# Sample-group scan step of a hybrid decoder: one decay multiply per half pinned in program order, and wider step spacing

## The chip, the cores and the metric

The kernel runs on one core of a Trainium2 chip. The metric is the device time of one execution in microseconds (us). It is written in a tile language: the program is traced into instructions for five engines, a scheduler then orders each engine's instructions by its own simulation of the time, and each engine works through its queue in that order. TensorE (PE) does matmuls, VectorE (DVE) and ScalarE (ACT) elementwise work, GpSimd (POOL) a little, and SyncE (SP) issues the DMAs.

## The reference

One step of a decoder trunk over 304 tokens: 16 meta tokens and 256 prompt tokens of one sequence, and 8 sample sequences of 4 tokens that carry a state.

```python
h = x + 0.5 * swiglu(rmsnorm(x), w_gu1, w_down1)
u = rmsnorm(h)
a_b, a_c, a_h, z, xbc, dt, g_a, g_b = split(u @ w_in)
y_a = (a_b * causal_conv3(a_c * a_h)) @ w_a_out
xs, bm, cm = split(silu(causal_conv4(xbc) + bias))
# per token t, for each of 32 heads (4 groups share bm, cm):
#   h_t = exp(dt_t * a) * h_{t-1} + dt_t * x_t * bm_t^T ;  y_t = h_t * cm_t
y_b = (rmsnorm_grouped((y + d_skip * xs) * silu(z))) @ w_b_out
h = h + (sigmoid(g_a) * y_a + sigmoid(g_b) * y_b) @ w_o
h = h + 0.5 * swiglu(rmsnorm(h), w_gu2, w_down2)
out = rmsnorm(h)          # and the new convolution and scan states
```

The scan of the 8 sample sequences is where the change lies: old states (8 x 32 heads x 64 x 128 numbers) are read, multiplied by a decay per head and sequence, and an update (an outer product of tokens and `bm`) is added.

## The kernel before, in words

**The weight stream.** All weights are streamed from memory in tiles of 128 x 128, eight tiles to a DMA (`wraw`). Each unit of eight is split into a high part (`whi`, by ACT, L183) and a low part (`wlo`, by DVE, L184), and each tile is used in three matmuls: high by high (L255), high by the low part of the activations (L258), low by high (L259). `PROGRAM`, an order written out by hand, says which tile comes when, and `drive` walks it. The results are named by phase: `ps_g`, `ps_u`, `ps_d` in the two feed-forward parts, and in the token mix `ps_x`, then `ps_ab`, `ps_ac`, `ps_ah`, and `ps_yb` and others later. When a row of `ps_ah` is done DVE multiplies it (`ab`, L530 and L531), convolves it (`cva`, L537, three times) and forms `yat` and `ya` (L544, L545, L548, with ACT between them).

**The scan beside it.** While phases `ab`, `ac`, `ah`, `z` and so on go through PE, two generators trace the scan in small steps: `prompt()` for the prompt's tokens, in eight parts of four heads, and `sample()` for the sample's, in four groups of eight heads, each of two halves (four sequences each). Both stand in a list `side`. After each weight tile `drive` adds `RATE2` = 0.36 to an account and advances one of the generators, in turn, for each whole step in it; a `yield` ends a step. So a `yield` alone issues nothing and only moves what is behind it later in the trace, by about three tiles per turn, twice that with two generators. While `sample()` sets `self.hold`, `prompt()` doesn't advance.

**What `sample()` does.** Per group g: the tokens are turned and scaled (`tokens(g)`: `xst`, `xdts`, `xl`), `diagonal(g)` multiplies a mask by them (L1146, `ms` by `xdts`). Then `cc` and `bm` are copied; eight products of the state tiles `h` with `cc` (both halves; L1183 before, L1185 after); ACT copies the result to `yr`; four transposes of `yr` (`K` by `yr`; L1191, L1194); DVE multiplies by `ec` into `yo` (L1196, L1199). Then for each half q: four decay multiplies `h = h * dec` (128 x 512 each, L1206, L1209), four `up` products into four PSUM tiles (L1220, L1225), four additions `h = up + h` (L1225, L1230), and the new state goes out by DMA (`store`, for the tile of an earlier half) and the one three halves later comes in (`load`). The `up` tiles of j = 1, 2, 3 take three of the four buffers of a PSUM tag "s", which all the scan's products `sps` share; that of j = 0 is in the pool of the weight stream.

**The prompt's products** in the same PSUM buffers: `xr` by `bt` (L1023, L1024), `xl` by `bl` (L1025), transposes of `xs` (L983), `xs` by `h` (L1043), `w` by `xd` (L1049). DVE reads them as `xd` and `xr` (L987), `hf` (L1029, L1031), `t` (L1052) and an update of `xs` (L1058).

**The order of the queues.** The scheduler may move an instruction ahead of others traced before it, but `tc.keep_in_program_order(ins)` holds `ins` behind everything traced ahead of it on its engine. Before the change it is used on PE: for each `up` product and, by `self.pin()`, for the next weight matmul, so that the weight stream can't pass the `up` products.

Of the kernel before, what the change touches and what calls it, by code (L numbers as in the profile page):

```python
# [12 lines left out]
ALU = mybir.AluOpType  # L13
# [695 lines left out]
class Scan:  # L709
# [375 lines left out]
    def sample(self):  # L1085
        nc, K, V, xs = self.nc, self.K, self.V, self.xs
        te, act, dve, pool = nc.tensor, nc.scalar, nc.vector, nc.gpsimd
        ident = K[:, C_ID:C_ID + P]
        NS = NB * NT
        NX = NS + NL  # L1090
        hts = {}

        def load(u):

            if u < 2 * G:
                hts[u] = self.t("h0", [P, 4, 512], bufs=3)
                nc.sync.dma_start(hts[u], self.h0[u // 2, u % 2])

        xst, rep, xt = {}, {}, {}
        yo = self.t("yo", [P, XC, NS])  # L1100
        late = []

        def tokens(g):


            hs = slice(8 * g, 8 * g + 8)

            def turned(src):
                p = self.ps()
                for j in range(4):  # L1110
                    te.transpose(p[:, j * P:(j + 1) * P], src[:, j], ident)
                return p.rearrange("p (h d) -> p h d", h=8)

            def decayed(pv, i, a):
                xr = self.t("xrs", [P, 8, HD], bufs=2, tag="tmp")
                dve.tensor_tensor(out=xr[a], in0=pv[a], op=ALU.mult,
                                  in1=self.dtr[a, i, hs].unsqueeze(2).to_broadcast([a.stop - a.start, 8, HD]))
                return xr.rearrange("p h d -> p (h d)")

            xf = decayed(turned(rep.pop(g)), 3, slice(0, P))  # L1120
            o = xst[g] = self.t("xst", [P, 512], bufs=2, dt=F32R)
            act.activation(o, xf, AF.Copy)
            dve.scalar_tensor_tensor(out=o, in0=xf, scalar=self.kd[:, 0:1], in1=o.bitcast(F32), op0=ALU.mult,
                                     op1=ALU.subtract)
            del xf
            m = self.mixed_rows(self.sp, 4 * g)
            yield
            pv = turned(m)
            del m
            xt[g] = self.t("xdts", [NX, 8, HD])  # L1130
            dve.tensor_tensor(out=xt[g], in0=pv[0:NX], op=ALU.mult,
                              in1=self.dt[0:NX, 2, hs].unsqueeze(2).to_broadcast([NX, 8, HD]))

            while self.xl:
                yield
            xf = decayed(pv, 2, slice(64, P))
            o = self.xl[g] = xlt
            act.activation(o[64:P], xf[64:P], AF.Copy)
            dve.tensor_tensor(out=o[96:P], in0=xf[96:P], in1=o[96:P].bitcast(F32), op=ALU.subtract)
            yield  # L1140

        def diagonal(g):
            pd = self.ps()
            for j in range(8):
                c, k = divmod(j, 2)
                te.matmul(pd[64 * k:64 * k + 64, c * NX:(c + 1) * NX], lhsT=xt[g][:, j],  # L1146
                          rhs=self.ms[:, 8 * g + j], start=True, stop=True)
            yd = self.t("yd", [P, 4, NX], bufs=2)
            act.activation(yd, pd[:, 0:4 * NX].rearrange("p (c t) -> p c t", c=4), AF.Copy)
            self.yd[g] = yd  # L1150

        def store():
            while late:
                u = late.pop()
                nc.sync.dma_start(self.o_hs[u // 2, u % 2], hts.pop(u))
                load(u + 3)

        for u in range(3):
            load(u)

        xlt = self.t("xl", [P, 512], dt=F32R)
        act.activation(xlt[0:64], K[0:64, 0:512], AF.Copy, scale=0.0)
        cc = self.t("cc", [P, 2 * (P + NT)])
        pool.memset(cc, 0.0)
        rep[0] = self.sample_rows(self.sp, 0)
        yield
        yield from tokens(0)
        diagonal(0)
        yield
        for g in range(G):  # L1170
            gs = slice(4 * g, 4 * g + 4)
            act.activation(cc.rearrange("p (q w) -> p q w", q=2)[:, :, 0:P].rearrange("p q (j r) -> p q j r", j=4)
                           [:, :, :, 0:NT],
                           xs[:, XC + G + g, S0:T].rearrange("p (q j t) -> p q j t", q=2, j=4), AF.Copy)
            bm = self.t("bm", [P, 2, P], dt=F32R)
            for q in range(2):
                act.activation(bm[:, q], self.bs[:, g].bitcast(F32), AF.Copy, scale=self.kd[:, 2 + q:3 + q])


            p = self.ps()  # L1180
            for q in range(2):
                for j in range(4):
                    te.matmul(p[32 * j:32 * j + 32], lhsT=cc[:, P * q + 32 * j:P * q + 32 * j + 32],  # L1183
                              rhs=hts[2 * g + q][:, j], start=q == 0, stop=q == 1)
            yr = self.t("yr", [P, 4, P], tag="tmp", bufs=2)  # L1185
            act.activation(yr, p.rearrange("p (c n) -> p c n", c=4), AF.Copy)
            yield
            store()
            p = self.ps()
            for c in range(4):  # L1190
                te.transpose(p[:, c * P:(c + 1) * P], yr[:, c], ident)  # L1191
            del yr
            for q in range(2):
                y, ec = (t[:, gs, 4 * NT * q:4 * NT * (q + 1)].rearrange("p c (b t) -> p c b t", b=4)  # L1194
                         for t in (yo, self.ec))
                dve.tensor_tensor(out=y, in0=p.rearrange("p (c b n) -> p c b n", c=4, b=4)[:, :, :, NT * q:NT * q + NT],  # L1196
                                  in1=ec, op=ALU.mult)
            if g + 1 < G:
                rep[g + 1] = self.sample_rows(self.sp, 4 * g + 4)  # L1199
            yield  # L1200
            for q in range(2):
                ht = hts[2 * g + q]
                for j in range(4):
                    oh = ht[:, j].rearrange("p (h d) -> p h d", h=8)
                    dec = self.dec[:, 8 * g:8 * g + 8, 4 * q + j].unsqueeze(2).to_broadcast([P, 8, HD])
                    dve.tensor_tensor(out=oh, in0=oh, in1=dec, op=ALU.mult)  # L1206
                    if j == 1:
                        yield

                self.hold = True  # L1210
                yield
                store()
                yield

                ps = [(self.pss if j else self.psm).tile([P, 512], F32, name=f"up{g}_{q}_{j}",
                                                        tag="s" if j else "m") for j in range(4)]

                for j in range(3, -1, -1):
                    a = slice(32 * j, 32 * j + 32)
                    ins = te.matmul(ps[j], lhsT=bm[a, q], rhs=xst[g][a], start=True, stop=True)  # L1220
                    self.tc.keep_in_program_order(ins)
                self.pin()
                self.hold = False
                for j in range(3, -1, -1):
                    dve.tensor_tensor(out=ht[:, j], in0=ps[j], in1=ht[:, j], op=ALU.add)  # L1225
                del ps
                yield
                yield
                late.append(2 * g + q)
                if q == 0:  # L1230
                    y = xs[:, gs, S0:T]
                    ds = V[:, V_DS + 4 * g:V_DS + 4 * g + 4].unsqueeze(2).to_broadcast([P, 4, NS])
                    dve.tensor_tensor(out=yo[:, gs], in0=yo[:, gs], in1=self.yd[g][:, :, 0:NS], op=ALU.add)
                    dve.tensor_tensor(out=y, in0=y, in1=ds, op=ALU.mult)
                    dve.tensor_tensor(out=y, in0=y, in1=yo[:, gs], op=ALU.add)
                    self.ready(g)
            if g + 1 < G:
                yield from tokens(g + 1)
                diagonal(g + 1)
                yield  # L1240
        store()
        yield
# [71 lines left out]
```

## Time and profile before

| what | value |
|---|---|
| runs, median of 3 | 886.96 us (886.14 to 887.67) |
| the profiled execution | 886.51 us |
| its span in the profile | 884.7 us |
| mean granted TensorE clock | 0.991 |
| PE busy | 866.3 us (98%) |
| DVE busy | 620.2 us (70%) |
| ACT busy | 491.1 us (56%) |
| POOL busy | 62.3 us (7%) |
| HBM read, written | 145.34 MB, 12.31 MB |

The span is the part of an execution that the profile's instructions cover; the profiled execution's own time is 1.81 us longer than it. PE is counted busy in 98% of the span, so what can be removed without taking matmuls away is in the few places where PE waits, and in stretches where its clock is granted lower than 1. Times within the trace are counted from the start of the span.

### The profile page before, as it was taken

The numbers are of one execution on the slowest core, as the hardware profiler recorded it, in microseconds if no ns is written. First come the engines' busy times: TensorE is split into PE (matmuls) and PEld (weight loads), VectorE is DVE, ScalarE is ACT, GpSimd is POOL, SyncE is SP. The second block draws the span as 40 slices with busy tenths as digits, with TensorE's granted clock in tenths as the row PEclk, the third lists the DMA queues.
The fourth block names the chain that finished last, engine by engine and source line by source line (L and its number), as shares of the span: only waits on it lengthen the run. The fifth ranks groups of instructions, "written<-read, shape, count | busy, mean of one in ns | idle before, by whom it ended". The sixth has DMA issues, their size and how long they took to land.

```text
span 884.7 us, 16212 instructions
## 1 busy us (share of the span) xinstructions
PE 866.3 (98%) x6428; PEld 845.8 (96%) x6428; DVE 620.2 (70%) x1002; ACT 491.1 (56%) x894; POOL 62.3 (7%) x87
## 2 busy tenths in 40 slices
PE   8999999999999999979999999999999999999995
PEld 7999999999999999869898989999999999999995
DVE  6766666554677798789999799796676666665443
ACT  7543434434677877845665676784465444444442
POOL 0000000000012372001000012100000000000000
PEclk9999999999999999989999999999999999999998
DMA  8554545555654655847584846555555555555541
GB/s 297 175 152 157 162 151 165 147 164 157 212 159 143 153 167 173 316 175 267 193 299 144 291 126 241 186 170 187 167 167 154 168 167 169 161 167 164 167 139 54
DMA packets 45851, 158.69 MB, mean 179 GB/s; under 512 B 7168, under 2 KB 9504, under 8 KB 43472
## 3 DMA queue, kind: packets, MB, share of 16 engines
q1 hardware_dynamic: 45344, 157.21, 55.3%
q8 instruction: 50, 0.82, 0.4%
q10 hardware_dynamic: 432, 0.46, 0.2%
q14 instruction: 25, 0.20, 0.1%
HBM read 145.34 MB, written 12.31 MB: 178 GB/s over the span
## 4 chain that ended last, share of the span: by engine, by line
PE 91%; ACT 4%; DVE 3%; issue 1%; DMA 1%; SPq 0%; DVEq 0%; ACTq 0%
PE ps_d L259 5%; PE ps_d L258 5%; PE ps_d L255 5%; PE ps_u L259 5%; PE ps_g L255 5%; PE ps_u L258 5%; PE ps_u L255 5%; PE ps_g L259 5%; PE ps_g L258 5%; PE ps_x L255 3%; PE ps_x L258 3%; PE ps_x L259 3%; PE ps_yb L259 2%; PE ps_yb L255 2%; PE ps_yb L258 2%; PE ps_z L255 2%
## 5 line engine op out<-in xcount | busy, mean ns | idle before, releaser
L184 DVE TENSOR_TENSOR wlo<-wraw,whi 128x1024 fp32r<-128x1024 f32 (+2 forms) x250 | 300.5, 1203 | 190.0 <-ACT whi L183 189.4
L183 ACT ACTIVATE whi<-wraw 128x1024 fp32r<-128x1024 f32 (+2 forms) x250 | 259.6, 1040 | 296.0 <-issue 183.9
L259 PE MATMUL ps_d<-hh,wlo 128*128 128x304 f32 (+1 forms) x352 | 105.6, 300 | 0.0
L255 PE MATMUL ps_d<-hh,whi 128*128 128x304 f32 (+1 forms) x352 | 105.0, 299 | 0.0
L258 PE MATMUL ps_d<-hl,whi 128*128 128x304 f32 (+1 forms) x352 | 104.7, 298 | 0.0
L258 PEld LDWEIGHTS ps_d<-hl,whi 128*128 128x128 f32 x352 | 66.7, 189 | 0.0
L259 PEld LDWEIGHTS ps_d<-hh,wlo 128*128 128x128 f32 x352 | 66.2, 188 | 0.0
L255 PEld LDWEIGHTS ps_d<-hh,whi 128*128 128x128 f32 x352 | 66.1, 188 | 0.0
L255 PE MATMUL ps_x<-unh,whi 128*128 128x304 f32 x192 | 58.9, 309 | 0.5 <-ACT dtraw L739 0.5
L258 PE MATMUL ps_x<-unl,whi 128*128 128x304 f32 x192 | 58.8, 306 | 0.0
L259 PE MATMUL ps_x<-unh,wlo 128*128 128x304 f32 x192 | 58.7, 306 | 0.0
L255 PE MATMUL ps_g<-n1h,whi 128*128 128x304 f32 x176 | 54.0, 307 | 1.4 <-ACT whi L183 1.4
L258 PE MATMUL ps_u<-n1l,whi 128*128 128x304 f32 x176 | 53.6, 304 | 0.0
L255 PE MATMUL ps_u<-n1h,whi 128*128 128x304 f32 x176 | 53.5, 304 | 0.0
L258 PE MATMUL ps_g<-n1l,whi 128*128 128x304 f32 x176 | 53.4, 304 | 0.0
L259 PE MATMUL ps_g<-n1h,wlo 128*128 128x304 f32 x176 | 53.1, 303 | 0.0
L259 PE MATMUL ps_u<-n1h,wlo 128*128 128x304 f32 x176 | 52.9, 302 | 0.0
L259 PE MATMUL ps_g<-n2h,wlo 128*128 128x288 f32 x176 | 52.3, 297 | 0.0
L255 PE MATMUL ps_u<-n2h,whi 128*128 128x288 f32 x176 | 52.2, 297 | 0.0
L259 PE MATMUL ps_u<-n2h,wlo 128*128 128x288 f32 x176 | 52.1, 296 | 0.0
L255 PE MATMUL ps_g<-n2h,whi 128*128 128x288 f32 x176 | 51.9, 295 | 0.0
L258 PE MATMUL ps_u<-n2l,whi 128*128 128x288 f32 x176 | 51.4, 292 | 0.0
(356 smaller groups left out, 2427.1 us busy)
## 6 DMA issues: line engine op xcount, KB each, us to landing
wraw<-wst SPq DMA_DIRECT2D x241, 512.0 KB, 3.6
h<-h SPq DMA_DIRECT2D x8, 1024.0 KB, 7.2
o_hs<-h SPq DMA_DIRECT2D x8, 1024.0 KB, 4.9
acb<-cumd SPq DMA_DIRECT2D x8, 512.0 KB, 5.1
wraw<-wst SPq DMA_DIRECT2D x7, 256.0 KB, 5.6
hd<-h SPq DMA_DIRECT2D x1, 1216.0 KB, 7.2
h<-hd SPq DMA_DIRECT2D x1, 1216.0 KB, 7.5
o_hp<-hf SPq DMA_DIRECT2D x8, 128.0 KB, 3.5
```

The source lines that it names most:

```text
L183: act.activation(hi[:, a:b], r[:, a:b], AF.Copy)
L184: dve.tensor_tensor(out=lo[:, a:b], in0=r[:, a:b], in1=hi[:, a:b].bitcast(F32), op=ALU.subtract)
L255: ins = te.matmul(o, lhsT=wh, rhs=xh, start=first, stop=False)
L258: te.matmul(o, lhsT=wh, rhs=xl, start=False, stop=False)
L259: te.matmul(o, lhsT=wl, rhs=xh, start=False, stop=last)
```

## The change

Two edits in `sample()`. The first decay multiply (j = 0) of each half is pinned on DVE behind everything traced ahead of it, 8 of 32 multiplies in all; the other three of each half are not. And there are more steps: one between `tokens(0)` and `diagonal(0)`, one more behind `diagonal(0)`, and in each of the four groups one between `store()` (behind the copy to `yr`) and the transposes of `yr`.

```diff
         yield from tokens(0)
+        yield
         diagonal(0)
+        yield
         yield
         for g in range(G):
...
             act.activation(yr, p.rearrange("p (c n) -> p c n", c=4), AF.Copy)
             yield
             store()
+            yield
             p = self.ps()
             for c in range(4):
                 te.transpose(p[:, c * P:(c + 1) * P], yr[:, c], ident)
...
                     dec = self.dec[:, 8 * g:8 * g + 8, 4 * q + j].unsqueeze(2).to_broadcast([P, 8, HD])
-                    dve.tensor_tensor(out=oh, in0=oh, in1=dec, op=ALU.mult)
+                    ins = dve.tensor_tensor(out=oh, in0=oh, in1=dec, op=ALU.mult)
+                    if j == 0:
+                        self.tc.keep_in_program_order(ins)
                     if j == 1:
                         yield
```

The number of instructions on each engine stays the same. In the rows below, numbers behind a name count the tiles of that name, `x8` stands for eight instructions in a row, and `up_0_3` is the product of group 0, half 0, j = 3.

PE's queue at group 0 before. These rows stand in one piece between two matmuls of the weight stream:

```order
L1146 MATMUL sps_4180<-ms_3023,xdts_4150 64x48 x8
L1183 MATMUL sps_4227<-h_29_4040,cc_4048 32x512 x4
L1183 MATMUL sps_4227<-h_30_4042,cc_4048 32x512 x4
L1191 MATMUL sps_4271<-K,yr_4236 128x128 x4
L1023 MATMUL sps_4297<-xr_4113,bt_4079 128x256
L1024 MATMUL sps_4297<-xr_4113,bt_4079 128x256
L983 MATMUL sps_4339<-K,xs 128x128 x4
L1220 MATMUL up_0_3_4405<-xst_4097,bm_4224 128x512
L1025 MATMUL sps_4297<-xl_4046,bl_3608 128x256
L1220 MATMUL up_0_2_4404<-xst_4097,bm_4224 128x512
L1220 MATMUL up_0_1_4403<-xst_4097,bm_4224 128x512
L1220 MATMUL up_0_0_4402<-xst_4097,bm_4224 128x512
```

PE's queue after, the first part. It now stands behind 21 matmuls of `ps_ah`, of which the first row shown is the last:

```order
L259 MATMUL ps_ah_4432<-unh,wlo_4310 128x290
L1146 MATMUL sps_4212<-ms_3023,xdts_4150 64x48 x8
L1023 MATMUL sps_4267<-xr_4113,bt_4079 128x256
L1024 MATMUL sps_4267<-xr_4113,bt_4079 128x256
L1185 MATMUL sps_4285<-h_29_4040,cc_4048 32x512 x4
L1185 MATMUL sps_4285<-h_30_4042,cc_4048 32x512 x4
L983 MATMUL sps_4322<-K,xs 128x128 x4
L255 MATMUL ps_ah_4432<-unh,whi_4309 128x290
```

The second part. It follows after 30 more weight matmuls (3 of `ps_ah`, 24 of `ps_ab`, 3 of `ps_ac`), with the product of `xl` by `bl` among them:

```order
L1043 MATMUL sps_4348<-xs,h_53_4265 128x144 x2
L1049 MATMUL sps_4347<-w_4165,xd_4112 64x112 x2
L1049 MATMUL sps_4347<-w_4165,xd_4112 64x144 x2
L1049 MATMUL sps_4347<-w_4165,xd_4112 64x112 x2
L1049 MATMUL sps_4347<-w_4165,xd_4112 64x144 x2
L1194 MATMUL sps_4383<-K,yr_4294 128x128 x4
L1225 MATMUL up_0_3_4521<-xst_4097,bm_4282 128x512
L1225 MATMUL up_0_2_4520<-xst_4097,bm_4282 128x512
L1225 MATMUL up_0_1_4519<-xst_4097,bm_4282 128x512
L1225 MATMUL up_0_0_4518<-xst_4097,bm_4282 128x512
L255 MATMUL ps_ac_4514<-unh,whi_4428 128x290
```

The transposes of `yr` and the `up` products moved 51 weight matmuls later, are still next to each other, and have the products L1043 and L1049 ahead of them, which stood behind them before.

DVE's queue at the same place before:

```order
L1206 TENSOR_TENSOR h_29_4040<-h_29_4040,dec_3029 128x512 x4
L544 TENSOR_TENSOR yat_4366<-ps_ab_4330,cva_4320 128x256
L545 TENSOR_TENSOR yat_4366<-ps_ab_4330,cva_4320 128x32
L1206 TENSOR_TENSOR h_30_4042<-h_30_4042,dec_3029 128x512 x4
L1196 TENSOR_TENSOR yo_4039<-sps_4271,ec_3031 128x4x16 x2
L987 TENSOR_TENSOR xd_4337<-sps_4339,dtt_2896 128x512
L987 TENSOR_TENSOR xr_4338<-sps_4339,dtr_3999 128x512
```

DVE's queue after, from the same `yat`. First the unpinned multiplies and what follows them:

```order
L545 TENSOR_TENSOR yat_4365<-ps_ab_4313,cva_4303 128x32
L548 TENSOR_TENSOR ya<-yat_4365,ya 128x288
L1209 TENSOR_TENSOR h_29_4040<-h_29_4040,dec_3029 128x512 x3
L1209 TENSOR_TENSOR h_30_4042<-h_30_4042,dec_3029 128x512 x3
L987 TENSOR_TENSOR xd_4320<-sps_4322,dtt_2896 128x512
L987 TENSOR_TENSOR xr_4321<-sps_4322,dtr_3999 128x512
L530 TENSOR_TENSOR ab_2513<-ps_ah_4432,act_4424 128x258
L531 TENSOR_TENSOR ab_2513<-ps_ah_4432,act_4424 128x8x4
L184 TENSOR_TENSOR wlo_4475<-wraw_4426,whi_4474 128x1024
L1029 TENSOR_TENSOR hf_4266<-h_53_4265,er_2975 128x256
L184 TENSOR_TENSOR wlo_4511<-wraw_4472,whi_4510 128x1024
L537 SCALAR_TENSOR_TENSOR cva_4468<-ab_2513,V,cva_4468 128x304
```

And directly behind that last row:

```order
L1058 SCALAR_TENSOR_TENSOR xs<-xs,V,sps_4347 128x256 x2
L1031 TENSOR_TENSOR hf_4266<-sps_4267,hf_4266 128x256
L1052 TENSOR_TENSOR t_64_4359<-sps_4348,eb_4232 128x288
L1199 TENSOR_TENSOR yo_4039<-sps_4383,ec_3031 128x4x16 x2
L1209 TENSOR_TENSOR h_29_4040<-h_29_4040,dec_3029 128x512
```

Six of the eight multiplies of group 0 still stand in one run ahead of `xd` and `xr`; the pinned one of the first half stands behind `yo`, and that of the second half 13 rows further on.

## The prediction

> **What bounds the kernel now.** I read the page's busy times and chain of waits first, then PE's waits, then windows around the one long wait, then the rows of PE and DVE in it.
>
> ```profile
> PE 866.3 (98%) x6428; PEld 845.8 (96%) x6428; DVE 620.2 (70%) x1002; ACT 491.1 (56%) x894; POOL 62.3 (7%) x87
> PE 91%; ACT 4%; DVE 3%; issue 1%; DMA 1%; SPq 0%; DVEq 0%; ACTq 0%
> ...
> PE up L1220 <- DVE yo L1196: 4.1, 1, 4.1
> PE ps_g L255 <- ACT whi L183: 1.4, 1, 1.4
> ...
> PE up L1220 <- DVE xr L987: 0.4, 1, 0.4
> ```
>
> PE carries 91% of the chain. Only what lets PE wait less, or run at full clock where it didn't, can bring time. The longest wait of PE is one of 4.1 us: an `up` product of group 0's first half waits for `yo` (its PSUM tile is the one that `yo` reads), and a shorter one waits for `xr`. The 1.4 us belong to the feed-forward part, which the change doesn't touch. So I look at that one place, by windows (PE, PEld, DVE, ACT, POOL busy, granted clock, DMA share, GB/s):
>
> ```profile
> 372.70:385.45 12.75, 6.87 (x51) 3.49 (x50) 12.59 (x24) 5.29 (x14) 1.06 (x1) 0.84 0.41 125
> 378.05:381.46 3.41, 1.43 (x8) 0.74 (x6) 3.38 (x8) 1.75 (x7) 0.00 (x0) 1.00 0.52 181
> 381.46:384.87 3.41, 0.90 (x3) 0.46 (x3) 3.41 (x9) 0.00 (x0) 0.00 (x0) 0.50 0.00 0
> 384.87:388.29 3.42, 3.42 (x14) 2.98 (x15) 3.42 (x9) 0.00 (x0) 0.00 (x0) 0.50 0.11 37
> 283.00:284.00 1.00, 1.00 (x6) 1.00 (x5) 0.00 (x0) 0.99 (x2) 0.00 (x0) 0.50 0.84 344
> 400.00:420.00 20.00, 20.00 (x155) 19.48 (x157) 18.21 (x34) 10.55 (x21) 1.73 (x4) 1.00 0.79 270
> ```
>
> From 372.70 to 385.45 no weight matmul runs, DVE is busy 12.59 of 12.75 us, and from 381.46 to 388.29 the granted clock is 0.50. That is the removable part. The rows of PE that mark it, and prices of the scan's products at full clock from the chain in order of time:
>
> ```profile
> 372.57 0.30 PE L259 MATMUL ps_ac<-unh,wlo 128*128 128x290 f32 x1
> 383.53 0.76 PE L1220 MATMUL up<-xst,bm 32*128 32x512 f32 x1 [4.05 <-DVE yo L1196]
> 384.73 0.79 PE L1220 MATMUL up<-xst,bm 32*128 32x512 f32 x2 [0.44 <-DVE xr L987]
> 385.45 0.61 PE L255 MATMUL ps_ah<-unh,whi 128*128 128x290 f32 x1
> 388.27 0.33 PE L259 MATMUL ps_ah<-unh,wlo 128*128 128x290 f32 x1
> 391.75 0.29 PE L255 MATMUL ps_ab<-unh,whi 128*128 128x288 f32 x1
> 395.34 0.30 PE L255 MATMUL ps_ac<-unh,whi 128*128 128x290 f32 x1
> ...
> 419.87 0.60 PE sps L1146 x16
> 420.83 1.85 PE sps L1183 x16
> 424.05 1.02 PE sps L1049 x16
> 425.67 0.44 PE sps L1191 x4
> 434.74 0.43 PE sps L1023 x2
> 445.61 0.49 PE sps L1043 x4
> ```
>
> In the hole stand diagonal .60, h·cc 1.85, two sets of four transposes .88, xr·bt .86, xl·bl and four `up` products (about .66 by the .44 for four products of that width): 4.85 us of work. So 12.75 − 4.85 = 7.9 us are idle. Behind it, the twelve weight matmuls that start from 385.45 to 388.27 are 2.82 us apart from first to last; 27 matmuls from 391.75 to 395.34 take 3.59, .133 each, so eleven steps would take 1.48: the half clock costs 1.3. Together 9.2 us are the most that this place can give.
>
> **The change, part by part.** DVE's rows at the place, for the walk:
>
> ```profile
> 374.11 1.23 DVE L184 TENSOR_TENSOR wlo<-wraw,whi 128x1024 fp32r<-128x1024 f32 x1
> 375.25 0.53 DVE L537 SCALAR_TENSOR_TENSOR cva<-ab,V,cva 128x304 f32<-128x304 f32 x1
> 375.69 1.22 DVE L184 TENSOR_TENSOR wlo<-wraw,whi 128x1024 fp32r<-128x1024 f32 x1
> 376.94 0.69 DVE L1139 TENSOR_TENSOR xl<-xrs,xl 32x512 fp32r<-32x512 f32 x1
> 377.66 2.50 DVE L1206 TENSOR_TENSOR h<-h,dec 128x512 f32<-128x512 f32 x4
> 380.19 0.42 DVE L544 TENSOR_TENSOR yat<-ps_ab,cva 128x256 f32<-128x256 f32 x1
> 380.75 0.44 ACT L547 ACTIVATE ya<-yat 128x288 fp32r<-128x288 f32 x1 [0.85 <-DVE yat L545]
> 383.04 0.34 DVE L1196 TENSOR_TENSOR yo<-sps,ec 128x64 f32<-128x64 f32 x2
> 383.30 0.68 DVE L987 TENSOR_TENSOR xd<-sps,dtt 128x512 f32<-128x512 f32 x1
> 383.90 0.68 DVE L987 TENSOR_TENSOR xr<-sps,dtr 128x512 f32<-128x512 f32 x1
> 384.50 0.41 DVE L1029 TENSOR_TENSOR hf<-h,er 128x256 f32<-128x256 f32 x1
> 385.43 0.45 DVE L548 TENSOR_TENSOR ya<-yat,ya 128x288 fp32r<-128x288 f32 x1
> 389.93 0.46 DVE L1052 TENSOR_TENSOR t<-sps,eb 128x288 f32<-128x288 f32 x1 [1.52 <-PE sps L1043]
> 391.10 0.87 DVE L1058 SCALAR_TENSOR_TENSOR xs<-xs,V,sps 128x256 f32<-128x256 f32 x2 [0.49 <-PE sps L1049]
> ```
>
> *The pin alone* moves 8 of 32 multiplies. One costs .62 (four in 2.50). In group 0 it takes two of the eight from ahead of `xd` and `xr`: 1.2 us; the other six stay there. The pinned one of half 0 stands behind `yo` and ahead of the first addition, so an addition waits for it, PE doesn't.
>
> *The extra steps* carry most. They let 21 weight matmuls pass ahead of diagonal, and 30 more pass ahead of the transposes of `yr`. PE, walked at .1345 a weight matmul of this stage (between .1325 for `ab` and .137 for the wider ones): 21 from 372.70 to 375.52, diagonal to 376.1, xr·bt to 377.0, h·cc to 378.8, transposes of xs to 379.3, 3 `ah` to 379.7, 24 `ab` and xl·bl to 383.07, 3 `ac` to 383.47, xs·h .49, w·xd 1.02 to 384.98, transposes of `yr` .44 to 385.42 (their PSUM buffer is free when `xr` is done). Then `up` 3 waits for the two updates of `xs` (L1058), `up` 2 for `hf` (L1031), `up` 1 for `t` (L1052), since these three now hold the PSUM buffers; and the pinned weight matmul stands behind them.
>
> When is DVE there? Its rows each overlap the next by some .07 us, so I take distances of starts. The order up to `xl` is the old one: 376.94 to 377.66. `yat` .34 and .10, with its end at 378.18; ACT's half of `ya` .44 and two handovers, to 378.66, for which DVE waits; `ya` .37 to 379.07; six multiplies at .61 to 382.73; `xd` and `xr` 1.2 (383.30 to 384.50) to 383.93; `ab` in two pieces like `yat`, .44, to 384.38; `wlo` 1.14 (374.11 to 375.25) to 385.52; `hf`'s first half .34 to 385.86; a second `wlo` to 387.0; `cva` .45 to 387.45; the two updates of `xs` .87 to 388.32. A wait on DVE costs .15 of handover (`yo` ends at 383.38, `up` starts at 383.53): `up` 3 at 388.47, behind `hf` at 388.8 `up` 2, behind `t` at 389.17 `up` 1, `up` 0 at once. The weight stream resumes at about 389.5.
>
> So the old wait, 7.9 us, is replaced by one of about 3.65: 385.42 to 388.47 in one piece, 3.05, and some .6 between the four `up` products. What is late now is no longer `yo` but the updates of `xs`, behind six multiplies and two `wlo`.
>
> *The sum.* By 389.5 PE has done all that it had done before at 395.34, when the first of the fourth group of three `ac` matmuls started: 5.84 us earlier, with no half clock in the new run. A new half-clock stretch is the one unknown cost. The windows of 3.41 us above show half clock in the window that follows one in which PE was busy 1.43 us, and again behind one with .90. In the same frame the window 384.87 to 388.29 of the new run would have PE busy .55 us, and half clock until 391.70; 2.2 us of weight stream from 389.5 at half clock lose 1.1, the `up` products a little. I take 1.2; its bounds are 0 (the frame lies otherwise, or the wait is too short) and 2.6 (twice the 1.3 seen). Gain 5.84 − 1.2 = 4.6. By sums, (7.9 + 1.3) − (3.65 + 1.2) = 4.35, which agrees.
>
> One rule bears on this: the Trainium skill, "TensorE: Matmul & The Clock Gate", section "HAM oscillation — how this bites in real kernels", wants no idle gap of TensorE above some 3.4 us, after which the clock falls to half. By that rule the new gap of 3.05 us costs no clock, and the gain would be the full 5.8 us.
>
> *Elsewhere* I cost the edits at nothing. In groups 1 to 3 and in the second halves, 38 to 80 rows of PE's queue lie between the transposes of `yr` and `up`, 5 to 10 us at .1325 to .137 each, against some 2.5 us for four multiplies: that cover hides the pinned one, and PE doesn't wait. The next critical `wlo` behind the pinned multiply and the additions is due about 3 us later than DVE reaches it. That cover is not endless: DVE is busy 18.21 of 20 us from 400 to 420. The state's DMAs behind `store()` go out a few tiles later on SP's queue:
>
> ```profile
> h<-h SPq DMA_DIRECT2D x8, 1024.0 KB, 7.2
> ...
> 392.12 0.34 SPq L1097 DMA_DIRECT2D h<-h  x1
> ```
>
> A load lands in 7.2 us; the first one of the scan is issued at 392.12 and read by the eight products of group 1 at 420.83, so some 20 us are to spare, and PE sees none of it.
>
> The profiled execution took 886.51, of which 884.7 is span: 886.51 − 4.6 = 881.9. It lies .45 below the median of 886.96, so the median after is 882.4.
>
> **Rivals.**
>
> *No half clock*: all as above, but the gap of 3.05 us leaves the clock alone: 886.96 − 5.84 = 881.1. For it speaks that the gap is shorter than the one before (4.05 us, and others ahead of it). Against it: at 283 the clock is .50 while PE is busy 1.00 of 1.00 us, so a long gap is not what it takes.
>
> *More gain*: DVE reaches the updates 3 us earlier than I walk, because the matmuls of `xs` by `h` and `w` by `xd` or the `wlo` come in another rhythm. Idle 1 us: 886.96 − 8.2 = 878.7. Against it: every price in DVE's walk has a row, and DVE has next to no idle time there.
>
> *Nothing comes of it*: what the change takes from DVE's queue is small, two multiplies, and the wait only moves from `yo` to the updates of `xs`. If DVE is 3 to 5 us later than walked (another `wlo` waits for its `whi`, or ACT's `ya` is late, with all six multiplies behind it), `up` starts at 392 to 393 and the gain is within 1.8 us of nothing: 885.2 to 888.7.
>
> *Slower*: the later groups have the same new order, and each stalls as group 0 does in its new place: 3.65 idle and 1.2 of clock, 4.85 each. With one, 886.96 − 4.6 + 4.85 = 887.2, the same as before; from the second on it is slower, 892.1. It decides where DVE falls behind by more than the 2 to 4 us that I count as cover at each such place. For it: 18.21 of 20 us busy. Against it: there, 38 to 80 rows of PE lie between, none in group 0.
>
> **The numbers.** The forecast, gain by a new, shorter wait with some half clock (881.7 to 884.2), has .55; without half clock .17; more gain .04; nothing or one later stall .14; two or more .10. A change of this kernel under 0.2% (1.8 us) can hardly be told from none, so faster means below 885.2 and slower above 888.7: .76, .14, .10. The range is 880.2 to 886.0: it leaves out the larger gain, most of the cases without gain and the slower ones, and takes in both bounds of the clock, 881.1 and 883.7, with about 2 us for DVE's walk on the side where it may be late and 1 us on the other.
>
> **What would show it.** Right: PE's waits list an `up` of about 3 us for the update of `xs`, L1058 (or `hf`, `t`), in place of 4.1 for `yo`; the stream of weights runs from 372.7 with no hole to about 385; `up` 0 is done at about 389.5; the granted clock is .50 for one window near 388 to 392; groups 1 to 3 have no new waits of PE above .5 us. Wrong: `up` later than 391 (DVE's walk failed), no half clock (the clock term), or PE waits for `wlo` or `up` behind 400 (the cover failed).

## The result, and the profile after

| kernel | median | runs | mean granted clock of the runs |
|---|---|---|---|
| before (with the change's own runs) | 886.71 us | 10 (885.23 to 887.67) | .991 over 43 runs of all comparisons |
| after | 881.65 us | 10 (879.43 to 884.48) | .995 (.991 to .998) |

The ratio is 0.9947, 95% interval 0.9933 to 0.9962: a gain of 0.4 to 0.7%, or 5.1 us by the medians. The forecast was 882.4 within 880.2 to 886.0. Measured once more beside other kernels (below), the changed kernel took 882.19 us against 885.84, a ratio of 0.9965 (0.9951 to 0.9980), and the forecast, a ratio of 0.9949, lies between these two; in us it is a little above both medians after. The profiled execution took 880.99 us, 5.52 less than the profiled one of before.

The page's busy times and the engines' shares of the chain after; then the waits of PE:

```profile
PE 863.8 (98%) x6428; PEld 843.6 (96%) x6428; DVE 619.8 (70%) x1002; ACT 491.7 (56%) x894; POOL 63.8 (7%) x87
...
PE 94%; DVE 2%; ACT 2%; issue 1%; DMA 1%; SPq 0%; POOLq 0%; POOL 0%; DVEq 0%; ACTq 0%
```

```profile
PE up L1225 <- DVE xs L1058: 2.4, 1, 2.4
...
PE sps L1043 <- ACT h L1028: 1.2, 1, 1.2
PE ps_g L255 <- ACT whi L183: 1.2, 1, 1.2
```

The span fell from 884.7 to 879.2. PE's time outside its busy rows fell by 3.0 us (18.4 to 15.4), its busy time by 2.5, in part because matmuls at half clock count as busy for longer. The wait for `yo` is gone, and in its place stands one of 2.4 us for the update of `xs`. A wait of 1.2 us is new; it lies at the end of the scan. The same windows as before, cut at the new hole (PE, PEld, DVE, ACT, POOL busy, granted clock, DMA share, GB/s):

```profile
372.70:385.45 12.75, 12.75 (x114) 10.17 (x112) 12.12 (x22) 6.62 (x13) 2.58 (x2) 1.00 0.42 125
385.45:388.89 3.44, 1.09 (x6) 0.55 (x5) 3.44 (x9) 3.43 (x10) 1.08 (x1) 1.00 0.71 189
388.89:396.00 7.11, 7.11 (x54) 7.00 (x52) 7.11 (x16) 3.72 (x11) 0.20 (x1) 1.00 0.65 251
400.00:420.00 20.00, 20.00 (x171) 17.46 (x170) 19.30 (x36) 14.75 (x35) 0.94 (x4) 1.00 0.84 301
```

Where PE had been busy 6.87 of 12.75 us, it is busy throughout; the hole is at 385.45, and in this execution the clock is 1.00 in it and behind it. PE's and DVE's rows at the place:

```profile
384.84 0.66 PE L1194 MATMUL sps<-K,yr 128*128 128x128 f32 x4
387.85 1.11 PE L1225 MATMUL up<-xst,bm 32*128 32x512 f32 x4 [2.35 <-DVE xs L1058]
388.89 0.40 PE L255 MATMUL ps_ac<-unh,whi 128*128 128x290 f32 x1
...
559.75 0.76 PE L1043 MATMUL sps<-xs,h 128*128 128x144 f32 x4 [1.20 <-ACT h L1028]
```

```profile
376.41 0.69 DVE L1139 TENSOR_TENSOR xl<-xrs,xl 32x512 fp32r<-32x512 f32 x1
378.54 3.70 DVE L1209 TENSOR_TENSOR h<-h,dec 128x512 f32<-128x512 f32 x6
382.15 0.69 DVE L987 TENSOR_TENSOR xd<-sps,dtt 128x512 f32<-128x512 f32 x1
...
386.38 0.54 DVE L537 SCALAR_TENSOR_TENSOR cva<-ab,V,cva 128x304 f32<-128x304 f32 x1
386.82 0.88 DVE L1058 SCALAR_TENSOR_TENSOR xs<-xs,V,sps 128x256 f32<-128x256 f32 x2
```

Against the walk: transposes of `yr` at 384.84 (walk 384.98), `up` 3 at 387.85 (388.47), the stream again at 388.89 (389.5). DVE was .5 ahead of the walk from `xl` on (376.41, walk 376.94), and stayed so. That lead is not of the change: the first of the transposes that read `mrows` (L1111), which stand ahead of the place in both orders, starts at 370.26 in this trace and at 370.78 in that of before. In a second profile of the changed kernel (below) it starts at 370.76, and there the transposes of `yr` come at 385.35, `up` 3 at 388.37 and the stream at 389.41. So DVE's part was walked right to .1 us, and PE came to the wait some .4 us later than walked, which makes the wait shorter.

### The profile page after: what moved, and what is told of

It reads as the page before. It is cut to its first block, busy times and chain, and to the rows that moved or that the text cites. A ratio compares the mean times of both kernels' runs of the same rounds, so it can differ in the third digit from the quotient of the medians.

```text
span 879.2 us, 16209 instructions
## 1 busy us (share of the span) xinstructions
PE 863.8 (98%) x6428; PEld 843.6 (96%) x6428; DVE 619.8 (70%) x1002; ACT 491.7 (56%) x894; POOL 63.8 (7%) x87
## 4 chain that ended last, share of the span: by engine, by line
PE 94%; DVE 2%; ACT 2%; issue 1%; DMA 1%; SPq 0%; POOLq 0%; POOL 0%; DVEq 0%; ACTq 0%
PE ps_d L259 6%; PE ps_d L258 5%; PE ps_d L255 5%; PE ps_u L259 5%; PE ps_g L255 5%; PE ps_u L258 5%; PE ps_u L255 5%; PE ps_g L259 5%; PE ps_g L258 5%; PE ps_x L255 3%; PE ps_x L258 3%; PE ps_x L259 3%; PE ps_yb L259 2%; PE ps_yb L255 2%; PE ps_yb L258 2%; PE ps_z L255 2%
```

## The experiments

Theory: the extra steps carry the gain, by letting weight matmuls pass ahead of products that wait for DVE; DVE's chain up to the update of `xs` sets what is left; the half clock behind a hole is a cost of its own. Rivals: the pin carries it; the half clock comes by itself; what is won is given back later. Each kernel was timed beside the kernel before on the same chip. The last column of the table below is 230 us less PE's busy time in the one window that holds the whole scan, from the profile of each kernel. The rows of that window, of before, where they give 6.3 us, and then of the full change, 3.6:

```profile
370.00:600.00 230.00, 223.73 (x1745) 207.58 (x1744) 205.44 (x366) 147.36 (x298) 19.87 (x24) 0.99 0.62 209
```

```profile
370.00:600.00 230.00, 226.37 (x1781) 211.08 (x1780) 208.06 (x372) 150.22 (x301) 22.72 (x23) 1.00 0.63 212
```

(A matmul that runs at half clock or waits for its operand within its row counts as busy, so this is less than the waits worked out by the prices of the products: 7.9 us in the one hole of before.)

The column "place" is the time from the first transpose of `mrows` to the start of the last matmul of `ps_yb`, behind the scan, in the same profile. By the traces every kernel has the same 2030 or 2031 matmuls there (18 more in the filled one), so it leaves out what differs elsewhere; before it is 267.8 us, with the full change 262.9. What lies ahead of it is the same program in all kernels, yet the profiles come to its start between 367.9 and 371.1 us. The medians hold such differences too, and one profile of a kernel doesn't tell whether they come by chance.

| kernel | median us | before, us | ratio (95% interval) | place, us | PE idle, 370 to 600, us |
|---|---|---|---|---|---|
| six steps, no pin | 882.07 | 886.40 | 0.9949 (0.9933 to 0.9964) | 265.7 | 3.7 |
| pin, no steps | 883.28 | 886.40 | 0.9969 (0.9958 to 0.9981) | 266.5 | 5.4 |
| pin and two steps at diagonal | 883.56 | 886.40 | 0.9966 (0.9952 to 0.9980) | 265.7 | 3.8 |
| pin and four steps behind store | 883.30 | 886.40 | 0.9959 (0.9944 to 0.9974) | 266.1 | 3.5 |
| before, its hole filled with matmuls | 883.05 | 885.83 | 0.9969 (0.9958 to 0.9980) | 266.4 | 2.5 |
| full change, one step ahead of up | 876.22 | 885.83 | 0.9890 (0.9875 to 0.9905) | 259.0 | 0.3 |
| full change, two steps ahead of up | 880.89 | 885.83 | 0.9943 (0.9930 to 0.9955) | 263.5 | 1.8 |
| full change, all four pinned | 877.87 | 885.83 | 0.9907 (0.9893 to 0.9920) | 261.5 | 1.3 |
| full change again | 882.19 | 885.84 | 0.9965 (0.9951 to 0.9980) | 263.0 | 3.7 |
| six steps, one ahead of up, no pin | 878.38 | 885.84 | 0.9914 (0.9898 to 0.9930) | 261.4 | 1.0 |
| one step ahead of up, all four pinned | 877.19 | 885.84 | 0.9902 (0.9886 to 0.9917) | 260.2 | 1.5 |

### The steps without the pin, the pin without the steps

The first takes the pin out of the changed kernel:

```diff
-                    ins = dve.tensor_tensor(out=oh, in0=oh, in1=dec, op=ALU.mult)
-                    if j == 0:
-                        self.tc.keep_in_program_order(ins)
+                    dve.tensor_tensor(out=oh, in0=oh, in1=dec, op=ALU.mult)
```

> The six extra steps without the pin. Theory (the steps carry the gain): PE's order around group 0 is the same as with both, and DVE does two more multiplies (1.2 us) but one cva less (.45) ahead of the updates of xs, and yo instead of hf behind them, so PE's wait for the first up product is 2.4 to 2.9 us instead of 2.35, and the median lies 0 to 1 us above that of the full change, 881.5 to 883 us. Rival (the pin carries it): the median is back within 1.5 us of before, above 885.

Its wait of PE, and three windows behind it:

```profile
PE up L1223 <- DVE xs L1058: 2.8, 1, 2.8
...
386.00:388.00 2.00, 2.00 (x7) 1.50 (x8) 2.00 (x7) 1.34 (x4) 0.00 (x0) 0.50 0.85 246
388.00:390.00 2.00, 2.00 (x10) 2.00 (x10) 2.00 (x5) 0.00 (x0) 0.00 (x0) 0.50 0.66 242
390.00:392.00 2.00, 2.00 (x10) 2.00 (x10) 2.00 (x5) 0.97 (x5) 0.30 (x1) 0.50 0.54 213
```

882.07 us, between the two medians of the full change (881.65, 882.19), with a wait .4 longer: by the medians the steps alone give the whole gain, and by the profile the whole of the idle time (3.7 us against 3.6). But here the half clock does follow the wait, for some 6.8 us, and the place is only 2.2 us shorter than before, against 4.9 with the full change. From the rows at half clock I estimate that it took 2.7 (21 weight matmuls from 387.33 to 392.56 in 5.23 us instead of 2.8, and the `up` products), which is the whole difference. Most of the rest of this execution's gain lies ahead of the place, which its trace reaches 2.8 us earlier. So the steps carry the idle time; that the full change was spared the half clock is not shown to be the pin's doing (see the clock rule below).

The second puts the pin alone into the kernel before, the same lines the other way.

> The pin without the extra steps. Theory: the hole of PE stays where it was, six multiplies instead of eight stand ahead of yo, so yo and with it up start 1.2 us earlier; the median falls by 1.2 us to 885.5, the half clock behind the hole stays. Rival (the pin carries it): 882 or less.

```profile
PE up L1222 <- DVE yo L1196: 2.9, 1, 2.9
...
382.00:384.00 2.00, 0.63 (x3) 0.38 (x3) 2.00 (x6) 0.00 (x0) 0.00 (x0) 0.97 0.00 0
384.00:386.00 2.00, 2.00 (x8) 1.56 (x9) 2.00 (x6) 0.00 (x0) 0.00 (x0) 0.50 0.00 0
386.00:388.00 2.00, 2.00 (x12) 2.00 (x12) 2.00 (x5) 0.00 (x0) 0.00 (x0) 0.68 0.18 63
```

The wait for `yo` fell by 1.2 us, as expected; the median fell by 3.1 (1.7 to 3.7 by the interval), not 1.2. The profiled execution (885.17) is the slowest of the twelve, and in it the place is 1.3 us shorter, as I said. The rest of the median goes with the clock, .9947 in the mean of the twelve runs against .9913, but this one profile doesn't show where: behind the hole half clock is one stretch of some 3.4 us where the kernel before had 6.8, and near 283 there is none, but one near 12 us. By the medians the pin adds nothing to the steps that these runs tell from zero. The two don't add up; that both shorten the same hole would explain it.

### Half of the steps

Two kernels take one group of steps out of the changed one; the first deletes the line between `store()` and the transposes, the second the two at diagonal:

```diff
             store()
-            yield
             p = self.ps()
```

> The pin and only the two steps around the first diagonal, not the four behind store(). Theory, by the walk of the queues: 33 instead of 51 weight matmuls pass ahead of up, PE is ready for up 2.4 us earlier than with the full change, at about 382.9, DVE's updates of xs are done at nearly the same time, so PE waits 4.5 to 5 us; the median is 2.1 us above the full change, 883.8, or up to 885 when half clock follows the longer wait. Rival (any one step is enough): as the full change, 881.5.

PE's waits of this kernel, as rows:

```profile
381.12 0.66 PE L1193 MATMUL sps<-K,yr 128*128 128x128 f32 x4 [0.52 <-ACT yr L1188]
383.48 1.09 PE L1049 MATMUL sps<-w,xd 128*64 128x112 f32 x16 [1.21 <-DVE xr L987]
385.65 0.46 PE L1224 MATMUL up<-xst,bm 32*128 32x512 f32 x1 [1.07 <-DVE yo L1198]
386.72 1.08 PE L1224 MATMUL up<-xst,bm 32*128 32x512 f32 x3 [0.61 <-DVE hf L1031]
```

883.56 against 883.8 expected, but not by the way that I gave: the waits come in pieces, 3.4 us in all where one of 4.5 to 5 was expected, and half clock for some 3.4 us follows them. And DVE's rows show a pinned multiply ahead of `yo`, seven multiplies of group 0 where only six are unpinned:

```profile
377.47 0.69 DVE L1208 TENSOR_TENSOR h<-h,dec 128x512 f32<-128x512 f32 x1 [0.18 <-PE sps L1185]
378.44 3.69 DVE L1208 TENSOR_TENSOR h<-h,dec 128x512 f32<-128x512 f32 x6
385.15 0.34 DVE L1198 TENSOR_TENSOR yo<-sps,ec 128x64 f32<-128x64 f32 x2
```

In the kernel's text the pinned multiplies of the group come behind `yo`, so the pin doesn't hold an instruction behind all that were traced ahead of it on its engine, as the description of the kernel has it. It would fit that the call ties it only to the one traced last on the same engine, so that it may run early where that one does; no run tries this.

> The pin and only the four steps behind store(), not the two around diagonal. Theory, by the walk: 18 weight matmuls pass ahead of diagonal, none stand between it and up; PE waits for yo at w times xd (2.4 us) and then for xr, hf and xs at the up products (about 2 us); the stream resumes at about 385.8, and the median is 1.3 us above the full change, 883, or 884 with a half clock. Rival (the steps behind store alone carry it): 881.5.

```diff
         yield from tokens(0)
-        yield
         diagonal(0)
-        yield
         yield
```

```profile
382.50 1.09 PE L1049 MATMUL sps<-w,xd 128*64 128x112 f32 x16 [2.13 <-DVE yo L1197]
384.54 0.79 PE L1223 MATMUL up<-xst,bm 32*128 32x512 f32 x1 [0.27 <-DVE hf L1031]
385.61 0.79 PE L1223 MATMUL up<-xst,bm 32*128 32x512 f32 x2 [0.29 <-DVE xs L1058]
```

883.30 against 883 to 884, the stream resumed at 386.33 (385.8 expected), and the wait for `yo` is 2.13 (2.4); half clock for some 6.8 us goes with it. Both kernels have the pin, and by their medians (883.56 and 883.30) neither is faster than the pin alone (883.28); in the place they are .8 and .4 us shorter than it, with half clock in all three profiles. So with the pin neither group of steps is shown to bring anything by itself; what the change has beyond the pin comes with all six.

### The half clock behind the hole

The kernel before, with matmuls that nobody reads in the wait:

```diff
+                    for _ in range(18 if (g, q, j) == (0, 0, 2) else 0):
+                        ins = te.matmul(ps[0], lhsT=bm[:, 0], rhs=xst[g], start=True, stop=True)
+                        self.tc.keep_in_program_order(ins)
                     ins = te.matmul(ps[j], lhsT=bm[a, q], rhs=xst[g][a], start=True, stop=True)
```

> The kernel before, with 18 extra matmuls (bm by xst, 128x512, written over by up 0 afterwards) in PE's queue between the up products that wait in group 0's first half: PE waits as long, but is busy in the wait. Theory (the hole costs twice: as idle time, and by the half clock that follows it): the stream of weights resumes at the same time, 385.5, but at full clock, and the median falls by 1.3 us (the 2.84 us of the stream at half clock in the profile) to 3 us (where the stretch lies later against the hole). Rival (half clock comes by itself, as at 283 where PE doesn't wait): no change, and .50 in the windows from 382 to 388.

```profile
377.12 2.58 PE L1221 MATMUL up<-xst,bm 128*128 128x512 f32 x10
379.66 2.00 PE L1221 MATMUL up<-xst,bm 128*128 128x512 f32 x8
382.75 0.49 PE L1223 MATMUL up<-xst,bm 32*128 32x512 f32 x2 [0.67 <-DVE xr L987]
383.17 0.40 PE L255 MATMUL ps_ah<-unh,whi 128*128 128x290 f32 x1
...
377.00:383.00 6.00, 5.33 (x23) 3.81 (x22) 5.97 (x13) 0.87 (x3) 0.00 (x0) 1.00 0.22 79
383.00:390.00 7.00, 7.00 (x60) 6.47 (x59) 5.80 (x14) 2.87 (x7) 0.20 (x1) 1.00 0.43 171
```

Added work made the kernel 2.8 us faster (1.8 to 3.7 by the interval). DVE is as busy as before in the hole (5.97 of 6.00), and the clock stays at 1.00 in it and behind it. So the rival, half clock by itself, is out for this place. By the trace the hole is .3 us shorter (12.46 from the last weight matmul to 383.17, against 12.75) and the 1.3 of the stream at half clock are gone, 1.6 us, and the place as a whole is 1.5 us shorter. The rest of the 2.8 this trace doesn't show in the scan: all stands 2 us earlier already ahead of the hole, for two reasons that lie outside the scan: the half-clock stretch at 283 is absent, as in seven of the eleven experiments' profiles, so that one does come and go by itself, and PE is busy 98.2 of the first 100 us instead of 97.3, a number that varies from 96.7 to 98.7 between the profiles.

The full change again, for its spread:

> The full change once more, beside the two kernels below on one chip. Its first profile shows PE's wait of 2.35 us at up and no half clock behind it; the steps-only kernel, with the same wait, shows half clock for 6.8 us right behind it. Theory (whether half clock follows a wait of this length changes from execution to execution): the same waits of PE, runs spread over 4 us and more, the short ones at a mean clock of .996 to .998, the long ones at .991 to .993; median 881 to 882.5. Rival (the spread has another source): runs at one clock differ as much as runs at different ones.

PE's wait was 2.4 us again, and again no half clock followed in the profiled execution:

```profile
388.37 1.11 PE L1225 MATMUL up<-xst,bm 32*128 32x512 f32 x4 [2.37 <-DVE xs L1058]
389.41 0.40 PE L255 MATMUL ps_ac<-unh,whi 128*128 128x290 f32 x1
```

The seven runs spread over 2.9 us, where 4 and more were expected; the 17 of both comparisons spread over 5. Five of them at a clock of .991 take 884.0 us on average, five at .996 take 881.6, two at .998 take 879.7. Fitted, .001 of mean clock goes with .55 us here and with .57 in 43 runs of the kernel before. So the spread goes with the clock. That half clock follows the hole in some executions only would fit it, but it isn't shown: both profiles of the full change have the stretch near 283, which the profiles of seven other kernels lack, and a run's mean clock doesn't tell the two apart. Nor does the changed kernel clearly spread more than the one before, whose 53 runs spread over 4.2 us.

### What is left of the wait

One step more, for the first half of group 0 alone, and two:

```diff
+                if (g, q) == (0, 0):
+                    yield
                 ps = [(self.pss if j else self.psm).tile([P, 512], F32, name=f"up{g}_{q}_{j}",
```

> The full change and one more step ahead of the up products of group 0's first half: 13 weight matmuls (1.74 us) now stand between them and the products ahead; DVE's order there is the same. Theory (what is left of the wait is DVE's updates of xs, which come no later): PE's wait of 2.35 us falls to 0.6, and with it the chance of half clock; median 1.7 to 2.5 us below the full change, 879.2 to 880. Rival (a later group or the end of the scan gives it back): 881.5 or more, with new waits behind 400.

```profile
PE 861.7 (99%) x6428; PEld 842.7 (97%) x6428; DVE 618.9 (71%) x1002; ACT 492.3 (56%) x894; POOL 59.7 (7%) x87
...
PE up L1227 <- DVE xs L1058: 0.3, 1, 0.3
```

876.22 us, the fastest kernel of this study, better than the 879.2 to 880 expected. The wait is .3 and there is none for L1043 at the scan's end: PE's idle time in the scan falls from 3.6 to .3. The place is 3.9 us shorter than with the full change. The rest of the 5.4 to 6.0 us against its two medians lies outside as far as the trace shows: it reaches the place 2.2 us earlier (368.05 against 370.26), ahead of all that the step touches.

> The same with two steps: 31 weight matmuls (4.1 us) ahead of the up products. Theory: no wait at up in group 0, 3.1 us of idle time gone, no half clock there; 878 to 878.8. Rival (given back later): 880 or more, with waits behind 400 or at the scan's end near 560.

```profile
PE ps_ya L255 <- ACT ya L547: 1.3, 1, 1.3
...
448.00:452.00 4.00, 2.65 (x18) 1.80 (x17) 2.83 (x7) 0.82 (x2) 0.00 (x0) 1.00 1.05 385
452.00:454.00 2.00, 2.00 (x10) 2.00 (x10) 2.00 (x4) 1.26 (x3) 0.00 (x0) 0.50 0.91 375
```

The wait at `up` is gone, and the rival came true: a new hole at 448 to 452 (PE busy 2.65 of 4.00 us), with half clock behind it, and 880.89 us; the place is .5 us longer than with the full change. A step ahead of `up` also moves everything of the scan behind it.

> The full change with all four decay multiplies of each half pinned. PE's order at group 0 stays; on DVE two instead of six stand ahead of xd and xr, but cva, yat and both wlo stand ahead of the updates of xs. Theory, by the walk: the updates are done at 386.5 instead of 387.7, up 0 at 387.2 instead of 388.9, and the median is 1.2 to 1.7 us below the full change, 880 to 880.5. Rival (later multiplies now stand ahead of what PE needs): 882 or more, with new PE waits for DVE.

```diff
-                    if j == 0:
+                    if True:
```

```profile
PE up L1225 <- DVE xs L1058: 0.7, 1, 0.7
PE ps_ya L255 <- ACT whi L183: 0.4, 1, 0.4
```

877.87 us, 3.8 to 4.3 below the full change where 1.2 to 1.7 were expected. The wait fell from 2.35 to .7 and idle time in the scan by 2.3, but the place is 1.5 us shorter, which is what was expected; the runs stand at a clock of .997, and this trace, too, reaches the place 2.2 us earlier. So the multiplies on DVE do hold up the update of `xs`.

The two together, and the one step without a pin:

> The six steps and the one step ahead of up in group 0, without any pin. In this order eleven weight matmuls come ahead of the transposes of yr, which are again next to up, and seven multiplies instead of six stand ahead of the updates of xs. Theory: PE is ready for up 1.5 us later than with the six steps alone, DVE's updates come at the same time, so the wait falls from 2.8 to about 1.3; 880 to 880.8. Rival (the pin is worth nothing once the step is there): as with the pin, 876.2.

878.38 us, better than the 880 to 880.8 expected; the waits at `up` are .7 and .2 where 1.3 was expected, and the pin's worth here, 2.2 us against 876.22, is no more than the two intervals allow to be chance.

> The six steps, the one step ahead of up in group 0, and all four multiplies of each half pinned. Theory: what the one and the other left of the wait, .3 and .7 us, is gone, no half clock in the scan; 875.5 to 876.5, the same as the better of the two or slightly better. Rival (both shift the later groups, and a new wait comes, as with two steps): 878 or more, with a wait behind 400.

877.19 us, above the 875.5 to 876.5 expected: no wait at `up` is left, but the rival's new wait is there, 1.0 us at 544, for POOL's `gacc` ahead of a product `g_ss`:

```profile
PE g_ss L282 <- POOL gacc L621: 1.0, 1, 1.0
```

## Why the prediction was right, point by point

- **Where the time lies.** Right: the hole of group 0's first half. Elsewhere PE's waits changed by 1.2 us (below) and by .4.
- **The walk of the queues.** Right: the new wait is for the update of `xs` as named, and the stream resumed at 388.89 and, in the profile without a lead, at 389.41 (389.5). Counted from the transposes of `mrows` that is 5.9 us earlier than before in both (5.84). The wait was 385.5 to 387.85, and the four products behind it took 1.04 us (1.03), of which .6 are idle: 2.95 us of idle time for 3.65, because PE's products ahead of it took longer than walked.
- **The steps carry most.** Shown for the idle time, by the kernel without the pin (3.7 us against 3.6). Its median (882.07) is that of the full change, but in its profile the place gains less, and more lies ahead of it.
- **The pin alone.** Its mechanism was right in group 0: 1.2 us of wait and 1.3 in the place. Alone its median gains 3.1 us; the rest goes with the clock of the runs, and where isn't shown.
- **The clock term.** Wrong for the profiled executions, and near the middle of what the clock can cost; the prediction itself named "no half clock" as the sign that this term failed. The old half clock, entered at 1.3, is caused by the hole, as the filled hole shows. The new one, entered at 1.2 for one window of 3.41 us, is 0 in two profiled executions of the full change and some 6.8 us long in that of the steps alone, where I estimate its cost at 2.7, just above the bound of 2.6; the runs' mean clocks, .991 to .998, may be the same mixture, together with the stretch near 283.
- **Elsewhere at nothing.** Nearly: groups 1 to 3 got no new wait, although DVE is busy 19.30 of 20 us from 400 to 420. But PE waits 1.2 us at 559.75 for the state copied by ACT, which I hadn't seen; the steps alone show it too (.8), either group of them alone doesn't, nor does the kernel with one step more, so it hangs on how the queues fall there; why is open. The term that speaks for this one in the prediction, the cover of later groups, didn't look past them.
- **Sum.** By prices, idle time is 7.9 − 2.95 − 1.2, and .4 for a wait for `wlo` that is gone: 4.15, and with 1.3 for the clock 5.45. The place became only 4.9 us shorter in both profiles of the change, so these prices are some .6 too high; that 5.45 is near the 5.52 between the profiled executions is luck, since .5 of those lie ahead of the place. The forecast's 4.6 is near 4.9 in part by luck, too: the half clock entered at 1.2 didn't come there, and the wait of 1.2 at the scan's end, entered at nothing, took as much. Between medians the gain is 5.1 in the first comparison and 3.85 over all runs (885.9 of 43, 882.05 of 17). The profiled execution's clock is .996 and the mean of the 17 runs .9941, which is 1.0 us by the slope above; how much of that is half clock behind the hole, and how much near 283, no run shows.
- **The rivals.** No half clock is what both profiled executions show, and not what the steps-only one does, so it may be a share of the runs and not a separate case. The larger gain (878.7) was reached only by other kernels. A stall of the later groups came with two steps ahead of `up`, not with the change.
- **The clock rule.** The section "HAM oscillation — how this bites in real kernels" of the page "TensorE: Matmul & The Clock Gate" in the Trainium skill wants gaps below some 3.4 us. Two profiles, with a wait of 2.4 us and 1.00 behind it, agree; the steps alone, with 2.8 us and .50 behind it, don't, and the kernel with one step and no pin still less. PE's two waits there, as rows, and the window behind them:

```profile
387.18 0.46 PE L1225 MATMUL up<-xst,bm 32*128 32x512 f32 x1 [0.73 <-DVE xs L1058]
387.87 0.86 PE L1225 MATMUL up<-xst,bm 32*128 32x512 f32 x3 [0.23 <-DVE hf L1031]
...
390.00:392.00 2.00, 2.00 (x10) 2.00 (x10) 2.00 (x5) 0.19 (x1) 0.00 (x0) 0.50 0.61 236
```

The walk carried the frame of windows of 3.41 us over from the trace of before, but each execution has its own. In a trace the edges of half clock are whole multiples of 3.41 us apart: 282.49, 285.91, 381.46, 384.87 and 388.29 before; 281.13, 284.54 and 875.05 after. Carried to the hole, the frame after has edges at 383.53, 386.94 and 390.35. The wait lies across one of them, and PE is busy 1.97 and 2.50 us in the two windows. In the steps-only kernel all but the last .3 us of the wait lies within the window that ends at 385.72, where half clock begins, and PE is busy .87 us in it. So where the hole falls in the frame may decide; it isn't the busy share alone, since with one step and no pin half clock follows a window with 2.45 us. No run moves the frame on purpose.

## What to carry to other kernels

When PE is the bound and waits for products of another engine, look for work of PE's own that may stand ahead of the wait; here 13 more weight matmuls ahead of four products (one step) gave 3.9 us in the scan on top of the change, and 31 lost that again at another place, so the rest of the schedule has to be read after each shift. Compare the stretch that was edited from one common instruction to another, as well as the whole time: here up to 3 us of difference lay ahead of everything that was edited. Price a hole of PE twice, as idle time and as half clock behind it, and look for the second in several executions, since one profile shows only one of its outcomes. A pin may hold an instruction behind less than its description says; look where it ran.

## What the hardware showed that I had not expected

Matmuls whose result nobody reads, put into a hole of 4 us, made the kernel 2.8 us faster by the medians and 1.5 in the scan, with the granted clock at 1.00 in the hole and behind it. And half clock followed PE's waits of .73 and .23 us in one execution, while it did not follow one of 2.4 us in two others.
